# Decoder layer, one core: weight parts made by adding transfers, and a new order of stages

## The chip, the cores and the metric

The kernel runs on one core of one Trainium2 chip. The metric is the device time of one execution in microseconds (us); lower is better. The engines are named as in the profile: PE (TensorE, matmuls), DVE (VectorE), ACT (ScalarE), POOL (GpSimd) and SP (SyncE, which here only issues transfers).

## What is computed

One decoder layer over 2048 tokens of width 1024, in float32. Three parts follow each other, each added to the residual stream:

```python
h = rms_norm(x, mix_norm_g); z = h @ w_in                    # 1024 x 2048
y_lru = rg_lru(causal_dwconv(lru_x, ...), ...) * gelu(lru_gate)
c     = silu(layer_norm(causal_dwconv(conf_a * sigmoid(conf_b), 31 taps)))
x = x + concat([y_lru, c]) @ w_out

q = rms_norm(x, xa_norm_g) @ w_q                             # 4 heads of 256
k, v = split(rms_norm(mem, mem_norm_g) @ w_kv)               # 256 memory tokens
x = x + (softmax(q k^T / 16) v) @ w_o

g, u = split(rms_norm(x, ffn_norm_g) @ w_up)                 # 2 x 3072
x = x + (gelu(causal_dwconv(g, 3 taps)) * u) @ w_down
return rms_norm(x, final_norm_g)
```

## The kernel before

**Arithmetic.** TensorE multiplies in a rounded float32 format (`F32R`). To keep the precision, each operand is held as two tiles: the high part, which is the value rounded to `F32R`, and the low part, which is the rest. `split` makes them (ScalarE copies to the high part, VectorE subtracts it from the source), and `mm3` does three matmuls: high by high, high by low, low by high. Nearly all tiles are 128 x 512.

**The layer's stages.** The 2048 tokens go in four quarters of 512. `mixer(q)` computes the two mixing branches, `normed(q)` the layer norm of the convolution branch, `attend(q)` the output projection, the attention over the memory tokens and its output. Since the memory is the same for all tokens, two products of weights are folded ahead: `memory_a` makes `A` from the keys and `w_q`, and `memory_vo` makes `VO` from the values and `w_o`. Both are kept in device memory as high and low parts (`A_rows`, `VO_rows`, tensors `A2` and `VO2`). `memory_vo` takes, for each of four heads, two blocks of 128 rows of `w_o`; each block is loaded at once (`raw_rows`, 512 KB) and its two halves are split.

Quarters 2 and 3 (`FOLDED`) go through `attend_pair`, which multiplies 2 x 2 blocks with seven products instead of eight (`Folded`). For that it needs sums and differences of weight blocks, which `Folds.prepare` makes ahead for `w_out`, `A` and `VO`. `Folds.block` fetches one block: for `w_out` it is loaded from the input; for the other two, the high and the low part are read back by `Rows.get` and VectorE adds them. The FFN works the same way on halves of 1024 tokens (`HalfX`, `strassen_cols`, `up`, `Down`), with operands named `B11`, `B21`, `T2`, and so on, in `UP_ORDER`. `first_x` rounds and splits the first `EARLY` of these seven sets ahead of the first weight column; the rest is made when a product first asks for it (`HalfX.get`).

**The order.** Nothing is ordered by hand at the level of instructions. Each stage is a generator (`Task`); `drive` steps the first task in the list that is due, where a `yield n` makes the task due again after TensorE has been given n us of further work. `TURNS` is the list, first come first; the constants beside it (`MEM_WAIT`, `MIX_WAIT`, `PAIR_WAIT`, `FOLD_PACE` and others) are those n. This gives the order of the matmuls and of the buffers. `Program` then plans all engines: `deadlines` works out from TensorE's order when each operation is due, `schedule` plays the program through with estimated costs (`estimate`, `HOP`, `DMA_DELAY`, `DMA_RATE`, `ISSUE`) and takes on each engine the ready operation that is due first, and `emit` writes the best of three passes. On the chip each engine and each transfer queue then runs its list in that fixed order. 84 tiles of 128 x 512 (`S`) are shared by all stages and are granted in the order of their creation.

All recorded operations carry the line of `emit` (L399), so groups are told apart by tile names: `wl<-raw,wh` is the low part of a weight, `wd<-wh,wl` the sum in `Folds.block`.

Of the kernel before, what the change touches and what calls it, by code (L numbers as in the profile page):

```python
# [48 lines left out]


HOP = 0.3
HOP_SAME = 0.1
DMA_DELAY = 2.5
DMA_RATE = 300e3
ACT_SWITCH = 1.3
ACT_PATIENCE = 8.0
POOL_LAST = 6.0
# [75 lines left out]
class Program:  # L133
# [68 lines left out]
        o.calls.append((name, (out,) + args, kw))  # L202
        self.touch(o, [r.buf for r in ins] + list(reads), [r.buf for r in outs] + list(writes))

    def dma(self, out, in_, reads=(), writes=(), join=False, slack=30, by="SP"):


        o = self.op(by)
        o.moves = True
        refs = [r for r in (out, in_) if isinstance(r, Ref)]  # L210
        nbytes = max(int(np.prod(r.dummy.shape)) for r in refs) * 4
        o.cost, o.delay = nbytes / DMA_RATE, DMA_DELAY
        o.calls.append(("dma_start", (), dict(out=out, in_=in_)))
        rd = [in_.buf] if isinstance(in_, Ref) else []
        wr = [out.buf] if isinstance(out, Ref) else []
        o.store = slack if rd else False
        self.touch(o, rd + list(reads), wr + list(writes), join)
# [42 lines left out]
    def schedule(self):  # L260
        events, seq = [], [0]
        ready = {e: [] for e in self.engines}
        busy = {e: 0.0 for e in self.engines}
        idle = {e: True for e in self.engines}
        free = {t: list(range(n)) for t, n in SLOTS.items()}
        queues = {t: list(reversed(q)) for t, q in self.queues.items()}
        table, dma_free, lag = [None], {e: 0.0 for e in ISSUE}, [0.0]
        order = []

        def push(t, kind, x):  # L270
            seq[0] += 1
            heapq.heappush(events, (t, seq[0], kind, x))

        def satisfied(o, t):
            o.at = max(o.at, t)
            o.wait -= 1
            if o.wait == 0:
                push(o.at, 1, o)

        def grant(tag, t):  # L280
            while free[tag] and queues[tag]:
                b = queues[tag].pop()
                b.slot = free[tag].pop(0)
                b.left = len(b.ops)
                for o in b.heads:
                    satisfied(o, t)

        def pick(e, t):
            h = ready[e]
            while h and h[0][2].start is not None:  # L290
                heapq.heappop(h)
            if not h:
                return None
            if e == "Pool":
                back, o, wake = [], None, None
                while h and o is None:
                    x = heapq.heappop(h)
                    if x[2].start is not None:
                        continue
                    spare = x[2].due + lag[0] - POOL_LAST - t  # L300
                    if x[2].either and spare > 0:
                        back.append(x)
                        wake = spare if wake is None else min(wake, spare)
                    else:
                        o = x[2]
                for x in back:
                    heapq.heappush(h, x)
                if o is None and wake is not None:
                    push(t + max(wake, 0.2), 3, e)
                return o  # L310
            if e == "ACT":
                o = h[0][2]
                if o.sets is not None and table[0] not in o.sets and o.due + lag[0] - t > ACT_PATIENCE:
                    other = [x for x in h if x[2].sets is None or table[0] in x[2].sets]
                    if other:
                        x = min(other)
                        h.remove(x)
                        heapq.heapify(h)
                        return x[2]
            return heapq.heappop(h)[2]  # L320

        def dispatch(e, t):
            if not idle[e]:
                return
            o = pick(e, t)
            if o is None:
                return
            idle[e] = False
            o.start, o.on = t, e
            order.append(o)  # L330
            if e == "PE":
                lag[0] += 0.2 * (t - o.turn - lag[0])
            cost = o.cost
            if e == "ACT" and o.sets is not None and table[0] not in o.sets:
                cost += ACT_SWITCH
                table[0] = o.sets[0]
            if o.either and e == "DVE":
                cost = estimate("DVE", "tensor_tensor", 1024, False)
            if o.moves:
                dma_free[e] = max(dma_free[e], t) + cost  # L340
                push(t + ISSUE[e], 2, e)
                push(dma_free[e] + o.delay, 0, o)
            else:
                push(t + cost, 2, e)
                push(t + cost, 0, o)

        for o in self.ops:
            o.wait = len(o.preds) + 1
        for tag, queue in self.queues.items():
            for b in queue:  # L350
                for o in b.heads:
                    o.wait += 1
        for tag in SLOTS:
            grant(tag, 0.0)
        for o in self.ops:
            satisfied(o, 0.0)
        end = 0.0
        while events:
            t, _, kind, o = heapq.heappop(events)
            end = max(end, t)  # L360
            if kind == 1:
                for e in (["DVE", "Pool"] if o.either else [o.eng]):
                    heapq.heappush(ready[e], (o.due, o.idx, o))
                    dispatch(e, t)
            elif kind == 3:
                dispatch(o, t)
            elif kind == 2:
                idle[o] = True
                dispatch(o, t)
            else:  # L370
                for s in o.succs:
                    satisfied(s, t + (HOP_SAME if s.eng == o.on else HOP))
                for b in o.bufs:
                    b.left -= 1
                    if b.left == 0:
                        free[b.tag].append(b.slot)
                        grant(b.tag, t + HOP)
        assert len(order) == len(self.ops)
        self.estimated = end
        return order  # L380
# [42 lines left out]
def hybrid_layer(  # L423
# [154 lines left out]
    def split(src, hi, lo):  # L578
        ACT(hi[:], src, AF.Copy)
        V("tensor_tensor", lo[:], src, hi[:].f32(), op=ALU.subtract)  # L580

    def split_scaled(src, g, hi, lo):
        ACT(hi, src, AF.Copy, scale=g)
# [440 lines left out]
    def memory_vo():  # L1024
        yield mem_a
        yield VO_LATE
        for h in range(4):
# [1 line left out]
            yield 1  # L1029
            pp = [ps() for _ in range(4)]  # L1030
            for db in range(2):
                st = raw_rows(w_o[0], h * M + db * P)
                ww = []
                for half in range(2):
                    hi, lo = pair("w")
                    split(st[:, half * TT : (half + 1) * TT], hi, lo)
                    ww.append((hi, lo))
                for i, p in enumerate(pp):
                    mb, (wh, wl) = i // 2, ww[i % 2]
                    vs = slice(db * M + mb * P, db * M + (mb + 1) * P)  # L1040
                    with together():
                        mm3(p[:], vh[:, vs], vl[:, vs], wh[:], wl[:], db == 0, db == 1)
                    if i % 2:
                        yield 0
# [609 lines left out]
    class Folds:  # L1654
# [5 lines left out]
        def block(self, k, half):  # L1660
            if self.rows.w is not None:
                t = tmp("wd")
                pr.dma(t[:], self.rows.w[k * P : (k + 1) * P, half * TT : (half + 1) * TT])
                return t
            hi, lo = self.rows.get(k, half)
            t = tmp("wd")
            V("tensor_tensor", t[:], hi[:].f32(), lo[:].f32(), op=ALU.add)
            return t

        def prepare(self, wait):  # L1670
# [302 lines left out]
        yield V_LATE  # L1973
        vec["v3072"] = columns([ffn_conv_w[0], ffn_conv_b], DFF, "v3072")

    EARLY, VO_WAIT, V_LATE, Z_COPIED = 5, 2, 500, (0, 1)
    MIX_WAIT, MIX_TURN, LN_SUM, LN_SQ, GATES = (5, 7, 6, 0), 5, 6, 0, 3
    MIX_PACE, ATT_PACE = (1, 4, 3, 4), ((0, 3, 0), (0, 2, 2), (6, 3, 3), (5, 9, 0))
    PAUSE, WARM = 2, 16
    FED = ("B21", "T2", "T1", "T3")  # L1980
    MEM_WAIT, VO_LATE, ATT_TURN, FFN_TURN, X_PACE, T_PACE = 17, 10, 1, (3, 8, 7, 24), 3, 10

    FOLDED = (2, 3)
    PAIR_WAIT, PAIR_TURN, FOLD_PACE = (0, 0, 9, 17), 7, (6, 7, 35)
    EARLY_AT, KEPT_AT = 6, 5
    FOLD_AT = lambda: ([turned_x[0]], [mem_a, turned_x[1]], [mem_vo])
    F_out, F_a, F_vo = Folds(W_out, "t_out"), Folds(A_rows, "t_a"), Folds(VO_rows, "t_vo")

    NORMED = [lambda: ([m[0]], 108), lambda: ([attended[0]], 31), lambda: ([m[2]], 26), lambda: ([m[3], n[2]], 6)]
    ATTEND = [lambda: [n[0]], lambda: [n[1]]]  # L1990
    TURNS = lambda: [later, first, fold, m[0], mem_a, m[1], first_t, a[0], n[2], m[3], n[0], n[3], mem_vo, n[1], m[2], a[1], a[2], tail]
    X = [HalfX(h) for h in range(NH)]

    def first_x():
# [6 lines left out]
    def feed_forward():  # L2001
        yield first
        yield attended[NQ - 1]
        spawn(X[1].kept(attends[NQ - 1], 20), tail)
        spawn(prepare_down(), tail)
        yield from up(0, X[0], X[1].make)
        down = Down()
# [55 lines left out]
```

## Time and profile before

| | us |
|---|---|
| median of 3 runs | 2397.39 (2396.77 to 2397.78) |
| profiled execution: span from first to last instruction | 2396.1 |
| PE busy | 2382.6 |
| DVE busy | 2034.0 |
| ACT busy | 1313.2 |
| POOL busy | 11.2 |

For the profiled execution no time is given beside its span; the span lies 1.3 us under the median of the timed runs and 0.7 us under the fastest. A group's row reads: line, engine, operation, written tile <- read tiles, shape and count | busy us, mean ns of one | idle time just before them and what ended it. A row of one tile gives the durations as min/median/max in ns, and the first and the last start in us. `SPq` and `POOL` rows with DMA are the issue of a transfer; the issue rows give count, KB each and the median time from issue to landing. The granted TensorE clock was 0.999 over the span. The transfers moved 604.56 MB.

### The profile page before, as it was taken

Reading aid. Unit: us, or ns where it says so; the run is one execution under the profiler, and the core shown is the slowest. Engines: PE = TensorE matmul, PEld = TensorE weight load, DVE = VectorE, ACT = ScalarE, POOL = GpSimd, SP = SyncE. Lnnn points to the kernel's source line nnn. Section 1 sums busy time; section 2 is a strip of 40 time slices with the busy share of each in tenths; the row PEclk is TensorE's granted clock in tenths of the full one; section 3 lists DMA queues with packets and bytes.
Section 4 is the critical chain, followed back from the end, with each engine's and each line's share of the span. In section 5 each row is a group of like instructions: output and inputs, shape, how many; then the busy total and the mean of one; then the engine's idle time right before and its main releaser. Section 6 shows DMA issues by size and latency. Waiting matters only on the chain.

```text
span 2396.1 us, 33483 instructions
## 1 busy us (share of the span) xinstructions
PE 2382.6 (99%) x10948; PEld 1974.5 (82%) x10948; DVE 2034.0 (85%) x3355; ACT 1313.2 (55%) x2374; POOL 11.2 (0%) x26
## 2 busy tenths in 40 slices
PE   9999999999999999999999999999999999999998
PEld 7898888888887888888888888888888888888887
DVE  7999994299899869879999887988988896676787
ACT  7772776357557678695555555554555541222333
POOL 1000000000000000000000000000000000000000
PEclk9999999999999999999999999999999999999999
DMA  9598789775878988787766544556565589887986
GB/s 351 197 296 309 234 300 305 254 255 176 296 261 271 318 277 280 268 289 265 252 234 208 194 172 158 175 177 211 190 216 199 186 303 324 283 280 254 312 303 258
DMA packets 363912, 604.56 MB, mean 252 GB/s; under 512 B 34809, under 2 KB 116985, under 8 KB 363738
## 3 DMA queue, kind: packets, MB, share of 16 engines
q1 hardware_dynamic: 362952, 601.81, 73.8%
q8 instruction: 86, 1.41, 0.2%
q14 instruction: 88, 0.72, 0.1%
q0 software_dynamic: 640, 0.36, 0.0%
q10 hardware_dynamic: 146, 0.27, 0.0%
HBM read 409.36 MB, written 192.94 MB: 251 GB/s over the span
## 4 chain that ended last, share of the span: by engine, by line
PE 94%; DVE 2%; ACT 2%; DMA 1%; issue 1%; SPq 0%; POOL 0%; DVEq 0%; POOLq 0%; ACTq 0%
PE ps L399 94%; DMA wl<-w_down 1%; DVE conv L399 1%; ACT L399 0%; DMA raw<-in_w_kv_dram 0%; ACT wh L399 0%; DVE wl L399 0%; ACT gate L399 0%; DVE x L399 0%; DVE s L399 0%; ACT yh L399 0%; DVE smalls L399 0%; DVE ptl L399 0%; ACT prob L399 0%; ACT conv L399 0%
## 5 line engine op out<-in xcount | busy, mean ns | idle before, releaser
L399 PE MATMUL ps<-Xh,wh 128*128 128x512 f32 x1344 | 523.3, 389 | 0.7 <-ACT u L399 0.7
L399 PE MATMUL ps<-Xh,wl 128*128 128x512 f32 x1344 | 523.2, 389 | 0.7 <-DVE wl L399 0.5
L399 PE MATMUL ps<-Xl,wh 128*128 128x512 f32 x1344 | 523.0, 389 | 0.0
L399 PE MATMUL ps<-wh,hidh 128*128 128x512 f32 x960 | 374.4, 390 | 0.0
L399 PE MATMUL ps<-wh,hidl 128*128 128x512 f32 x960 | 374.2, 390 | 0.1
L399 PE MATMUL ps<-wl,hidh 128*128 128x512 f32 x960 | 373.7, 389 | 0.0
L399 DVE SCALAR_TENSOR_TENSOR conv<-cb,v,conv 128x512 f32<-128x512 f32 x480 | 334.9, 741 | 1.8 <-ACT conv L399 0.9
L399 PEld LDWEIGHTS ps<-Xh,wl 128*128 128x128 f32 x1344 | 252.3, 188 | 54.0 <-DVE wl L399 1.5
L399 PEld LDWEIGHTS ps<-Xh,wh 128*128 128x128 f32 x1344 | 252.3, 188 | 53.1 <-ACT u L399 1.1
L399 PEld LDWEIGHTS ps<-Xl,wh 128*128 128x128 f32 x1344 | 252.3, 188 | 52.5
L399 ACT ACTIVATE hidh<-s 128x512 fp32r<-128x512 f32 x186 | 113.8, 631 | 271.6 <-DVE s L399 227.9
L399 PEld LDWEIGHTS ps<-wh,hidl 128*128 128x128 f32 x960 | 180.2, 188 | 39.5 <-DVE hidl L399 2.1
L399 PEld LDWEIGHTS ps<-wh,hidh 128*128 128x128 f32 x960 | 180.2, 188 | 37.8 <-ACT hidh L399 0.4
L399 PEld LDWEIGHTS ps<-wl,hidh 128*128 128x128 f32 x960 | 180.3, 188 | 37.2 <-DMA wl<-w_down 0.4
L399 PE MATMUL ps<-xh,wh 128*128 128x512 f32 x512 | 204.0, 398 | 0.1
L399 PE MATMUL ps<-xl,wh 128*128 128x512 f32 x512 | 199.6, 390 | 0.3 <-DVE xl L399 0.3
L399 PE MATMUL ps<-xh,wl 128*128 128x512 f32 x512 | 199.6, 390 | 0.0
L399 ACT ACTIVATE wh<-s 128x512 fp32r<-128x512 f32 x192 | 119.6, 629 | 117.6 <-DVE s L399 79.1
L399 ACT ACTIVATE wh<-raw 128x512 fp32r<-128x512 f32 (+2 forms) x214 | 127.4, 613 | 53.1 <-PE ps L399 21.6
L399 ACT ACTIVATE u<-ps 128x512 f32<-128x512 f32 x144 | 85.7, 595 | 126.0 <-PE ps L399 125.2
L399 DVE TENSOR_TENSOR acc<-acc,ps 128x512 f32<-128x512 f32 (+1 forms) x157 | 102.7, 678 | 59.5 <-PE ps L399 56.4
L399 DVE TENSOR_TENSOR wl<-raw,wh 128x512 fp32r<-128x512 f32 (+2 forms) x214 | 140.2, 668 | 12.0 <-ACT wh L399 10.7
(256 smaller groups left out, 4014.2 us busy)
## 6 DMA issues: line engine op xcount, KB each, us to landing
raw<-in_w_up_dram SPq DMA_DIRECT2D x96, 512.0 KB, 4.5
wh<-w_down SPq DMA_DIRECT2D x156, 256.0 KB, 4.9
wl<-w_down SPq DMA_DIRECT2D x156, 256.0 KB, 5.0
w_down<-wh SPq DMA_DIRECT2D x144, 256.0 KB, 3.1
w_down<-wl SPq DMA_DIRECT2D x144, 256.0 KB, 3.5
h<-hid SPq DMA_DIRECT2D x120, 256.0 KB, 4.7
wh<-w_in SPq DMA_DIRECT2D x96, 256.0 KB, 4.2
wl<-w_in SPq DMA_DIRECT2D x96, 256.0 KB, 4.7
```

The costliest lines, as they stand in the source:

```text
L399: getattr(e, name)(*[resolve(a) for a in args], **{k: resolve(a) for k, a in kw.items()})
```

## The change

Three things:

1. In `memory_vo`, `split` of a loaded block of `w_o` becomes `split_fetched`. A transfer issued by POOL writes the high part directly from the input (rounding on the way), ScalarE writes its negative to the low part, and a second transfer from POOL adds the input to that. VectorE and the loaded copy have no part in it any more.
2. In `Folds.block`, for `A` and `VO`, the high part is read to the target by SP, and the low part is added to it by a transfer from POOL. Before, VectorE added two tiles that had been read.
3. The planner's transfers share one estimated stream with a delay of 3.5 us (it was one stream for each issuing engine, 2.5 us); and `TURNS` and the constants beside it have other values.

```diff
-HOP_SAME = 0.1
-DMA_DELAY = 2.5
-DMA_RATE = 300e3
+HOP_SAME = 0.05
+DMA_DELAY = 3.5
+DMA_RATE = 350e3
...
-    def dma(self, out, in_, reads=(), writes=(), join=False, slack=30, by="SP"):
+    def dma(self, out, in_, reads=(), writes=(), join=False, slack=30, by="SP", **more):
...
-        o.calls.append(("dma_start", (), dict(out=out, in_=in_)))
+        o.calls.append(("dma_start", (), dict(out=out, in_=in_, **more)))
...
-                dma_free[e] = max(dma_free[e], t) + cost
+                dma_free[0] = max(dma_free[0], t) + cost
                 push(t + ISSUE[e], 2, e)
-                push(dma_free[e] + o.delay, 0, o)
+                push(dma_free[0] + o.delay, 0, o)
...
+    def split_fetched(hi, lo, src):
+        pr.dma(hi[:], src, by="Pool")
+        ACT(lo[:], hi[:].f32(), AF.Copy, scale=-1.0)
+        pr.dma(lo[:], src, by="Pool", accum_op=ALU.add)
...
             for db in range(2):
-                st = raw_rows(w_o[0], h * M + db * P)
+                r0 = h * M + db * P
                 ww = []
                 for half in range(2):
                     hi, lo = pair("w")
-                    split(st[:, half * TT : (half + 1) * TT], hi, lo)
+                    split_fetched(hi, lo, w_o[0][r0 : r0 + P, half * TT : (half + 1) * TT])
...
-            hi, lo = self.rows.get(k, half)
+            kept, i = self.rows.kept, (k * 2 + half) * 2
             t = tmp("wd")
-            V("tensor_tensor", t[:], hi[:].f32(), lo[:].f32(), op=ALU.add)
+            pr.dma(t[:], kept.at(i), reads=[kept.tok[i]])
+            pr.dma(t[:], kept.at(i + 1), reads=[kept.tok[i + 1]], by="Pool", accum_op=ALU.add)
             return t
...
-    EARLY, VO_WAIT, V_LATE, Z_COPIED = 5, 2, 500, (0, 1)
-    MIX_WAIT, MIX_TURN, LN_SUM, LN_SQ, GATES = (5, 7, 6, 0), 5, 6, 0, 3
-    MIX_PACE, ATT_PACE = (1, 4, 3, 4), ((0, 3, 0), (0, 2, 2), (6, 3, 3), (5, 9, 0))
-    PAUSE, WARM = 2, 16
+    EARLY, VO_WAIT, V_LATE, Z_COPIED = 1, 1, 500, (0, 1)
+    MIX_WAIT, MIX_TURN, LN_SUM, LN_SQ, GATES = (3, 7, 10, 0), 5, 5, 0, 3
+    MIX_PACE, ATT_PACE = (2, 4, 3, 4), ((0, 3, 2), (0, 2, 2), (0, 0, 0), (0, 0, 0))
+    PAUSE, WARM = 1, 16
...
-    MEM_WAIT, VO_LATE, ATT_TURN, FFN_TURN, X_PACE, T_PACE = 17, 10, 1, (3, 8, 7, 24), 3, 10
+    MEM_WAIT, VO_LATE, ATT_TURN, FFN_TURN, X_PACE, T_PACE = 5, 11, 4, (6, 10, 0, 0), 0, 12
...
-    PAIR_WAIT, PAIR_TURN, FOLD_PACE = (0, 0, 9, 17), 7, (6, 7, 35)
+    PAIR_WAIT, PAIR_TURN, FOLD_PACE = (1, 0, 16, 36), 7, (8, 6, 35)
...
-    NORMED = [lambda: ([m[0]], 108), lambda: ([attended[0]], 31), lambda: ([m[2]], 26), lambda: ([m[3], n[2]], 6)]
+    NORMED = [lambda: ([m[0]], 108), lambda: ([attended[0]], 32), lambda: ([m[2]], 27), lambda: ([m[3], n[2]], 18)]
...
-    TURNS = lambda: [later, first, fold, m[0], mem_a, m[1], first_t, a[0], n[2], m[3], n[0], n[3], mem_vo, n[1], m[2], a[1], a[2], tail]
+    TURNS = lambda: [n[3], later, m[0], n[1], fold, mem_a, m[1], n[2], n[0], a[0], m[3], first, mem_vo, m[2], a[1], first_t, a[2], tail]
...
-        spawn(X[1].kept(attends[NQ - 1], 20), tail)
+        spawn(X[1].kept(attends[NQ - 1], 43), tail)
```

More of the change, by code (lines that the diff above doesn't have):

```diff
@@ L266, in schedule @@
         queues = {t: list(reversed(q)) for t, q in self.queues.items()}
-        table, dma_free, lag = [None], {e: 0.0 for e in ISSUE}, [0.0]
+        table, dma_free, lag = [None], [0.0], [0.0]
         order = []
```

## The prediction

> **What bounds the kernel now.** I read the page first, then busy time by stage, then what TensorE waited for. From the page: the span, the busy rows, and VectorE's slices (busy tenths, forty equal ones).
>
> ```profile
> span 2396.1 us, 33483 instructions
> PE 2382.6 (99%) x10948; PEld 1974.5 (82%) x10948; DVE 2034.0 (85%) x3355; ACT 1313.2 (55%) x2374; POOL 11.2 (0%) x26
> DVE  7999994299899869879999887988988896676787
> ```
>
> TensorE (PE) is busy in 2382.6 of 2396.1 us, so 13.5 us are all that any reordering can touch. By stretch (start:end, length, then busy us of PE, PEld, DVE, ACT, POOL, the granted clock, the transfer engines' share, GB/s):
>
> ```profile
> 0.00:2.41 2.41, 0.00 (x1) 0.01 (x1) 0.39 (x6) 1.10 (x1) 1.45 (x8) 1.00 0.09 25
> 2.41:60.00 57.59, 57.31 (x288) 47.77 (x289) 46.73 (x105) 43.08 (x90) 9.73 (x19) 1.00 1.03 365
> 60.00:300.00 240.00, 238.50 (x1217) 203.22 (x1216) 236.85 (x373) 145.29 (x265) 0.00 (x0) 1.00 0.77 259
> 300.00:360.00 60.00, 59.31 (x280) 48.09 (x279) 58.68 (x93) 46.11 (x83) 0.00 (x0) 1.00 0.87 302
> 700.00:780.00 80.00, 79.48 (x370) 63.67 (x369) 79.06 (x130) 66.66 (x113) 0.00 (x0) 1.00 0.81 276
> 1480.00:1530.00 50.00, 48.62 (x213) 39.27 (x212) 46.78 (x76) 32.58 (x55) 0.00 (x0) 1.00 0.55 184
> 2300.00:2389.50 89.50, 89.40 (x391) 72.68 (x389) 73.63 (x141) 38.48 (x89) 0.00 (x0) 1.00 0.82 302
> 2389.50:2396.13 6.63, 0.00 (x1) 0.00 (x0) 1.96 (x6) 2.03 (x6) 0.00 (x0) 0.77 0.42 158
> ```
>
> The first 2.41 us and the last 6.63 us hold no matmul, and the change edits neither. That leaves 13.5 - 2.4 - 6.6 = 4.5 us of idle TensorE in the middle: 0.28, 1.50, 0.69, 0.52, 1.38 and 0.10 us in the six stretches shown between, and 0.04 in the others. The waits of TensorE (writer, what it waited for, us, times, longest) name them; the first lies at the start:
>
> ```profile
> PE ps L399 <- POOL ident masks.py:199: 2.4, 1, 2.4
> PE ps L399 <- DMA raw<-in_w_kv_dram: 1.5, 1, 1.5
> PE ps L399 <- ACT u L399: 0.7, 1, 0.7
> PE ps L399 <- DVE wl L399: 0.5, 1, 0.5
> PE ps L399 <- DVE x L399: 0.5, 1, 0.5
> PE ps L399 <- DVE xl L399: 0.3, 1, 0.3
> PE ps L399 <- ACT prob L399: 0.3, 1, 0.3
> PE ps L399 <- DVE ptl L399: 0.2, 1, 0.2
> ```
>
> Where the first two of the middle lie, by the chain that ended last (start, length):
>
> ```profile
> 137.94 7.47 DMA raw<-in_w_kv_dram
> ...
> 353.30 0.61 DVE x L399
> ```
>
> These are slightly short of the truth. Matmuls start every 0.23 us and are recorded as 0.39 us long, so each wait can hide another 0.16 us. Timeline rows (start, length) of two matmuls and of the transfer that the first needs, and the same for the first use of the output weights; all serve below:
>
> ```profile
> 239.24 0.42 SPq L399 DMA_DIRECT2D raw<-in_w_o_dram  x1
> 252.68 0.39 PE L399 MATMUL ps<-wh,kvh 128*128 128x512 f32 x1
> 252.91 0.39 PE L399 MATMUL ps<-wl,kvh 128*128 128x512 f32 x1
> ...
> 159.62 1.07 SPq L399 DMA_DIRECT2D raw<-in_w_o_dram  x2
> L399 PE MATMUL ps<-wh,kvh x32: 389/389/390, 181.7 to 373.8; 128*128 128x512 f32 x32
> ```
>
> For the seven waits of the middle that is 7 x 0.16 = 1.1 us. All that can be won is about 4.5 + 1.1 = 5.6 us, 0.23% of the run. VectorE (DVE) is nearly as full as TensorE in 60-360 and 700-780 us (236.85 of 240, 58.68 of 60, 79.06 of 80), so its work can come late there; that is where the edit takes work from it.
>
> **The change, part by part.** (1) The output weights `w_o`. Four heads, two row blocks, two halves: 16 splits. Each loses a VectorE subtraction; its ScalarE copy stays as a copy scaled by -1; and 8 loads of 512 KB on SP become 32 transfers of 256 KB on POOL, half of them adding to their target. (2) The sums of kept parts of `A2` and `VO2`: 32 blocks, each losing a VectorE addition and one of two SP transfers, for one adding transfer on POOL. The rows: a subtraction like the 16, the 32 additions, the loads of w_o, a kept part, and what POOL has moved so far.
>
> ```profile
> L399 DVE TENSOR_TENSOR wl<-raw,wh 128x512 fp32r<-128x512 f32 x43 | 28.0, 681 | 0.6 <-ACT wh L399 0.5
> L399 DVE TENSOR_TENSOR wd<-wh,wl x32: 672/681/693, 609.0 to 963.3; 128x512 f32<-128x512 f32 x32
> raw<-in_w_o_dram SPq DMA_DIRECT2D x8, 512.0 KB, 6.7
> wl<-A SPq DMA_DIRECT2D x60, 256.0 KB, 4.9
> tmp<-in_lru_w_x_dram POOLq DMA_DIRECT2D x2, 64.0 KB, 5.9
> 12.70 1.25 POOL L399 DMA_DIRECT2D tmp<-in_lru_w_x_dram  x2
> ```
>
> VectorE is relieved of 48 x 0.68 = 33 us in all: 16 x 0.68 = 10.9 us ahead of 360 us, and 32 x 0.68 = 21.8 us spread over 609-963 us, of which 700-780 gets about 21.8 x 80 / 354 = 4.9 us. The bytes of w_o double, 4 MB more on some 605, where the transfer engines run at 0.77: nothing on the path unless the chain below is late.
>
> The price of the first part is a longer chain. Now it is load (6.7), copy (0.6), subtraction (0.7): 8.0 us. Afterwards it is rounding load, negating copy, adding load. No row shows an adding transfer or a 256 KB transfer by POOL. The nearest is POOL's 64 KB at 5.9 us, beside SP's 256 KB at 4.9, so 5.9 + 0.6 + 5.9 = 12.4 us. POOL takes 0.63 us to issue a transfer of 64 rows (1.25 for two); for 128 rows I take twice that, 1.3 us, and if it isn't within the 5.9 the chain is 15.0 us. Behind the adding transfer, which waits on POOL's queue for the copy, stand only the next w_o load and the sums, since POOL's list ends at 14 us today. 64 x 1.3 = 83 us of issue is no load in 2396. The tightest lead in the rows above, issue to matmul, is 252.68 - 239.24 = 13.4 us; the first loads, at 159.6 us, lead by 22 (181.7). So the chain fits at 12.4 and misses by 1.6 at 15.0; the planner counts POOL's issue and 3.5 us of delay, and can ask earlier. I take 0, between 0 and the price of the last rival. For the sums nobody hurries: they feed a product that is stored and read later. They cost nothing, and they free two of three tiles per block.
>
> [...]
>
> (3) The order. `MEM_WAIT` goes from 17 to 5, so the memory's keys and values start up to 12 us earlier, before the transfers of 120-200 us fill up; there the one wait on `w_kv` arose (1.5 us visible, 1.7 with its hidden part). Between all of it and none I take half: -0.8. `DVE x` at 354 us (0.5, 0.7 with the hidden part) follows directly on the 10.9 us of relief: all gone, -0.7. `ACT prob` and `DVE ptl` (0.3 and 0.2, with hidden 0.8) lie in 700-780, where 4.9 us of VectorE are freed: gone, -0.8. What is late next there is VectorE again, only less. The 1.38 us of 1480-1530 come from rounding the second half's activations during the last weights of the first half; nothing in the edit relieves that: 0. POOL's and SP's queues are passed by the moved tasks too, but 40 fewer SP issues leave room.
>
> `EARLY` goes from 5 to 1: of seven sets of rounded activations for the FFN, only one is asked for ahead of its first weight column. Each set is four splits, so up to 16 splits may move past the FFN's start at 1042.8 us.
>
> ```profile
> 1020.00:1043.00 23.00, 23.00 (x120) 19.60 (x119) 18.50 (x31) 22.19 (x45) 0.00 (x0) 1.00 0.72 256
> 1043.00:1063.00 20.00, 20.00 (x107) 17.09 (x106) 12.17 (x22) 18.78 (x36) 0.00 (x0) 1.00 0.89 299
> L399 DVE TENSOR_TENSOR Xl<-tx,Xh x16: 659/684/693, 1024.5 to 1054.3; 128x512 fp32r<-128x512 f32 x16
> L399 DVE TENSOR_TENSOR Xl<-xn,Xh x12: 681/683/693, 1013.0 to 1061.1; 128x512 fp32r<-128x512 f32 x12
> L399 PE MATMUL ps<-Xh,wh x1344: 388/389/500, 1042.8 to 1962.0; 128*128 128x512 f32 x192
> L399 ACT ACTIVATE wh<-s 128x512 fp32r<-128x512 f32 x192 | 119.6, 629 | 117.6 <-DVE s L399 79.1
> ```
>
> Here ScalarE is the tight one: 18.78 of 20 us, with 1.2 free. Sixteen copies of 0.63 us are 10.1, so 8.9 us uncovered if all of them move; none if the planner, which may run them as soon as tiles are free, leaves them where they are. The nearest case is the second half's set, made on the fly, at 1.38 us. I take half of that, +0.7, since the stage ahead is looser than the one at 1480.
>
> Sum: -0.8 - 0.7 - 0.8 + 0.7 = -1.6 us on the profiled 2396.1, so a span of 2394.5. The median of the runs, 2397.39, stands 1.3 above that profile; the prediction is 2397.39 - 1.6 = 2395.8 us.
>
> **The rivals.** *Waits change places.* A new order of 18 tasks and some 30 numbers removes the eight waits and makes eight others. For it: VectorE stays over 90% full in 60-300 after the relief (236.85 - 10.9 = 226 of 240), and the waits are single events of 0.2 to 1.5 us. The relief then isn't seen: 2397.4, give or take 1.5.
>
> *All waits go.* 2397.39 - 5.6 = 2391.8 us. Against it: more than half of the 5.6 lies at 145 us (a transfer) and at 1480-1530, where the edit takes nothing off an engine.
>
> *The FFN starts late* (slower). The mechanism is `EARLY`; the place is 1043-1063 us; the price reaches 8.9 us instead of 0.7: 2395.8 + 8.2 = 2404.0. It decides from 16 x 0.63 - 1.2 down to about 7.2 us uncovered (then the other gains no longer hold the total within 0.2%), that is, when some 13 of the 16 splits really move. Against it: the 28 splits of the seven sets already reach from 1013 to 1061 us today, ahead of and behind the start, with no wait of TensorE.
>
> *POOL's chain is late* (slower too). At 15.0 us, and behind one more issue of 1.3, a group with the tightest lead waits 2.9 us. If four of the eight groups have that lead, 11.6 us: 2407.4. It decides from about 6.5 us in all.
>
> Would a full VectorE hold POOL's issues up? At 12.70-13.95 us POOL issued at 0.63 us each beside a VectorE that ran the forms with two tensors which fill it where w_o is fetched:
>
> ```profile
> 11.99 1.41 DVE L399 SCALAR_TENSOR_TENSOR xl<-ps,vmix,xh 128x512 fp32r<-128x512 f32 x2 [0.34 <-ACT xh L399]
> 13.32 0.41 DVE L399 TENSOR_TENSOR wl<-raw,wh 128x256 fp32r<-128x256 f32 x1
> ```
>
> [...]
>
> **How the numbers follow.** A difference under 0.2% (4.8 us) can hardly be told from no change. Chances: the forecast 0.41, waits change places 0.28, all waits go 0.12, FFN late 0.11, POOL late 0.08. Faster by over 0.2% (below 2392.6) is only the third: 0.12. Slower (above 2402.2) is the last two, less 0.01 for a part that stays small: 0.18. The same: 0.70. The range goes from 2391.7 (all waits gone) to 2404.0 (FFN late in full); outside it remain POOL's chain and as much again for waits that I cannot name. The likeliest case alone is 2393.5 to 2397.5.
>
> **What would show it.** Right: VectorE's busy time about 33 us lower, as many matmuls as before, POOL with 64 more transfers; no wait on `DVE x` near 354 us or at 700-780; TensorE idle in the middle about 3 us. Wrong: TensorE waiting for `wl` or `wh` of w_o behind a transfer or ScalarE's negation near 160-375 us (POOL's chain); waits on `Xh` or `Xl` in the 20 us after the FFN's start (EARLY); adding transfers that land much later than 6 us; waits of a microsecond or more in stages that the edit doesn't touch, which would mean that the order, and not the transfers, made the time.

## The result, and the profile after

The changed kernel takes 2401.92 us (median of 21 runs, 2398.10 to 2406.06), the kernel before, timed beside it, 2397.39 (2395.80 to 2399.05). The ratio is 1.0019, interval 1.0013 to 1.0026: 4.5 us slower, where 1.6 us faster was forecast. Its runs spread over 8 us, those of the kernel before over 3.3. The profiled execution took 2398.55 us (span 2396.8), so it is one of the shorter ones: some 3.4 us of the median are not in it. A second profiled execution (e4 below) is 2.1 us longer.

From the page of the changed kernel, the span and the busy row:

```profile
span 2396.8 us, 33552 instructions
PE 2382.4 (99%) x10948; PEld 1975.9 (82%) x10948; DVE 2008.4 (84%) x3307; ACT 1303.1 (54%) x2368; POOL 62.5 (3%) x90
```

VectorE has the 48 instructions fewer that were forecast, POOL 64 transfers more, TensorE the same 10948. Busy time by stage, columns as in the prediction:

```profile
120.00:200.00 80.00, 80.00 (x490) 72.69 (x489) 79.01 (x124) 44.59 (x93) 8.99 (x13) 1.00 0.99 314
250.00:300.00 50.00, 48.74 (x220) 39.03 (x220) 49.84 (x79) 41.67 (x73) 0.00 (x0) 1.00 0.66 216
300.00:360.00 60.00, 60.00 (x285) 49.22 (x284) 54.09 (x85) 42.34 (x82) 5.78 (x8) 1.00 0.97 324
700.00:780.00 80.00, 77.92 (x356) 62.96 (x353) 71.46 (x117) 66.05 (x109) 4.37 (x5) 0.98 0.84 280
1043.00:1063.00 20.00, 20.00 (x106) 17.11 (x105) 14.20 (x25) 16.64 (x32) 0.00 (x0) 1.00 0.93 328
1480.00:1530.00 50.00, 50.00 (x223) 41.39 (x222) 45.02 (x74) 31.76 (x53) 0.00 (x0) 1.00 0.52 179
```

Three of the old holes are gone: the one at 145 us, the one at 354, and the 1.38 us of 1480-1530, which nothing was expected to touch. In 700-780 VectorE went from 79.06 to 71.46 us, and yet TensorE's idle time there went from 0.52 to 2.08. A new hole is in 250-300 (1.26 us). The same stretch of the kernel before was full:

```profile
250.00:300.00 50.00, 50.00 (x228) 40.45 (x227) 49.29 (x78) 40.43 (x70) 0.00 (x0) 1.00 0.74 239
```

What TensorE waited for in the changed kernel (the wait for `x` is new too and lies in the first 30 us; those for `xl` and `vol` are the hole in 250-300):

```profile
PE ps L399 <- POOL ident masks.py:199: 2.5, 1, 2.5
PE ps L399 <- DVE ptl L399: 2.1, 1, 2.1
PE ps L399 <- DMA x<-in_x_dram: 0.8, 1, 0.8
PE ps L399 <- DVE xl L399: 0.7, 1, 0.7
PE ps L399 <- DVE vol L399: 0.5, 1, 0.5
```

The wait of 2.1 us lies at 756 us. TensorE's rows there, and the six microseconds around them by busy time and clock:

```profile
755.04 1.03 PE L399 MATMUL ps<-ident,prob 128*128 128x128 f32 x8
758.16 1.11 PE L399 MATMUL ps<-ident,prob 128*128 128x128 f32 x4 [2.08 <-DVE ptl L399]
758.93 0.78 PE L399 MATMUL ps<-wh,pth 128*128 128x512 f32 x1
...
757.00:763.00 6.00, 4.84 (x19) 4.03 (x20) 3.60 (x6) 5.92 (x7) 0.72 (x1) 0.72 1.07 354
```

The wait costs twice. After it the granted clock is 0.72 over six microseconds, and matmuls of 512 columns, which start every 0.23 us ahead of the wait (753.45, 753.68), start every 0.43 us until about 761.5. The trace has the clock at one half for 3.41 us (0.50 from 758.11 to 761.52), so by estimate half of that, about 1.7 us, is lost on top of the 2.08. ScalarE's list in the same place shows what `ptl` (the low part of a turned probability, which needs the high part `pth`) waits for:

```profile
753.58 0.63 ACT L399 ACTIVATE m<-m 128x512 f32<-128x512 f32 x1
754.23 1.28 ACT L399 ACT_TABLE_LOAD   x1
755.52 0.72 ACT L399 ACTIVATE gate<-gate,nsp 128x512 f32<-128x512 f32 x1
756.15 0.61 ACT L399 ACTIVATE m<-xc 128x512 f32<-128x512 f32 x1
756.79 1.08 ACT L399 ACTIVATE pth<-ps 128x512 fp32r<-128x512 f32 x2
757.89 1.28 ACT L399 ACT_TABLE_LOAD   x1
```

The first four transposes end at about 755.6; the copy of their result starts at 756.79, behind a table load and two activations of a gate. TensorE's next transposes wait 2.08 us for `ptl`, which reads that result too (the bracket in their row). The engine that is late is ScalarE, which is busy only 66.05 of 80 us: it seems to have the wrong order and not too much work, which h1 below tests.

The transfers, by count, size and median time from issue to landing:

```profile
wh<-in_w_o_dram POOLq DMA_DIRECT2D x16, 256.0 KB, 6.7
wl<-in_w_o_dram POOLq DMA_DIRECT2D x16, 256.0 KB, 7.3
wd<-A POOLq DMA_DIRECT2D x16, 256.0 KB, 5.9
wd<-VO POOLq DMA_DIRECT2D x16, 256.0 KB, 7.5
...
L399 POOL DMA_DIRECT2D wl<-in_w_o_dram x16 | 14.3, 949 | 30.6 <-ACT wl L399 17.2 <-ACT ctail L399 7.4 <-ACT cb L399 5.9
```

### The profile page after: what moved, and what is told of

It is laid out like the page before. It is cut to its first block, busy times and chain, and to the rows that moved or that the text cites. A ratio compares the mean times of both kernels' runs of the same rounds, so it can differ in the third digit from the quotient of the medians.

```text
span 2396.8 us, 33552 instructions
## 1 busy us (share of the span) xinstructions
PE 2382.4 (99%) x10948; PEld 1975.9 (82%) x10948; DVE 2008.4 (84%) x3307; ACT 1303.1 (54%) x2368; POOL 62.5 (3%) x90
## 4 chain that ended last, share of the span: by engine, by line
PE 91%; DVE 6%; DMA 1%; ACT 1%; issue 1%; SPq 0%; POOL 0%; DVEq 0%; POOLq 0%; ACTq 0%
PE ps L399 91%; DVE conv L399 4%; DMA x<-in_x_dram 0%; DMA wd<-VO 0%; DVE al L399 0%; DVE qtl L399 0%; DVE xl L399 0%; SPq L399 0%; ACT gate L399 0%; DVE vol L399 0%; ACT L399 0%; DVE kvl L399 0%; DVE gate L399 0%; DVE xc L399 0%; DVE smalls L399 0%
## 5 line engine op out<-in xcount | busy, mean ns | idle before, releaser
L399 DVE TENSOR_TENSOR wl<-s,wh 128x512 fp32r<-128x512 f32 x192 | 130.0, 685 | 15.3 <-ACT wh L399 9.5
L399 ACT ACTIVATE wh<-raw 128x512 fp32r<-128x512 f32 (+2 forms) x198 | 117.6, 612 | 43.1 <-PE ps L399 17.1
L399 DVE TENSOR_TENSOR wl<-raw,wh 128x512 fp32r<-128x512 f32 (+2 forms) x198 | 130.1, 668 | 10.8 <-ACT wh L399 10.6
```

Source lines behind the costliest of these rows:

```text
L399: getattr(e, name)(*[resolve(a) for a in args], **{k: resolve(a) for k, a in kw.items()})
```

## The experiments

The change has three parts: the planner's numbers (`HOP_SAME`, `DMA_DELAY`, `DMA_RATE`, one estimated stream), the order of stages (`TURNS` and the constants beside it), and the transfers. The first runs take them apart. Below, *lost time* over a stage is worked out from the starts of the matmuls: how much the distances from one to the next exceed the usual distance of that kind in the kernel before, added up. It holds waits and slow clock alike. How much it is depends on what is called usual; its differences between runs are good to about half a microsecond.

**e1_order_only**: the changed kernel with the old data path.

```diff
-                    split_fetched(hi, lo, w_o[0][r0 : r0 + P, half * TT : (half + 1) * TT])
+                    split(st[:, half * TT : (half + 1) * TT], hi, lo)
...
-            pr.dma(t[:], kept.at(i + 1), reads=[kept.tok[i + 1]], by="Pool", accum_op=ALU.add)
+            V("tensor_tensor", t[:], hi[:].f32(), lo[:].f32(), op=ALU.add)
```

> The changed kernel's order of stages and planner numbers, with the old data path: w_o loaded and split with VectorE, the kept parts summed by VectorE, no adding transfer. Theory 1 (the new order made the time, the adding transfers are free): 2400 to 2404 us, ratio to the kernel before 1.0012 to 1.0027, single runs spread over 6 us or more as in the changed kernel (2398.1 to 2406.1). Theory 2 (the adding transfers land at varying times and hold something up): 2394 to 2398 us, runs spread over no more than 4 us as before (2395.8 to 2399.1).

Measured: 2406.39 us (2403.29 to 2406.97), ratio 1.0035 (1.0021 to 1.0049). That is above both expectations. New order and new numbers alone cost 9.0 us; the transfers then give 4.5 back.

**e2_transfers_only**: the kernel before with both kinds of adding transfer, old order, old numbers (the diff's `split_fetched` and `Folds.block`, nothing else).

> The kernel before with both kinds of adding transfers and nothing else (old order of stages, old planner numbers). Theory 1: 2394 to 2398 us, spread up to 4 us. Theory 2: 2400 us or more, spread 6 us or more; the old planner assumes a delay of 2.5 us for a transfer that takes 6 to 7, so it would be worse than the changed kernel.

Measured: 2432.08 us (2429.19 to 2439.04), ratio 1.0150 (1.0136 to 1.0164). By themselves the transfers cost 34.7 us. The waits of ScalarE and TensorE name a cause:

```profile
ACT wl L399 <- DMA wh<-in_w_o_dram: 46.7, 12, 11.1
...
PE ps L399 <- DVE xl L399: 8.4, 5, 3.5
PE ps L399 <- ACT xh L399: 6.5, 3, 3.6
```

ScalarE's negating copy (`wl`) waits 46.7 us for POOL's load. TensorE does not wait for `wh` or `wl` of `w_o` at all; it waits for activations that have nothing to do with `w_o`.

**e3_wo_by_vector**: the changed kernel, but `w_o` is split by VectorE as before; only the sums are made by transfers.

> The changed kernel with w_o loaded and split by VectorE again; the sums of kept parts still by adding transfers. Theory 1: as the changed kernel, 2400 to 2404 us. Theory 2, the w_o chain being what holds up (wl of w_o lands 7.3 us after issue, twice in a row): 2394 to 2398 us. Theory 2, the sums being what holds up: 2400 us or more.

Measured: 2402.07 us (2400.95 to 2406.24), ratio 1.0022 (1.0012 to 1.0032). By the medians the sums by transfer gain 4.3 us against e1 (the two intervals overlap); against the changed kernel, `w_o` by transfer gains nothing that can be told from zero.

**e4_changed_again**: the changed kernel once more, beside e1 to e3.

> The changed kernel, for a second profiled execution: the one shown took 2398.55 us and the median was 2401.92, so the typical execution's extra 3.4 us are not in that trace. Both theories: median 2400 to 2404 us. Theory 1: the extra is a wait of TensorE for VectorE or ScalarE, followed by matmuls at half the clock, as at 757-763 us. Theory 2: a wait within 20 us behind a transfer issued by POOL.

Measured: 2401.36 us (2397.03 to 2404.35), ratio 1.0015 (1.0006 to 1.0024). Its profiled execution, 2.1 us longer than the other, has the wait for `ptl` at 2.7 us and one more, of 1.4 us for `xh`, at 261 us:

```profile
761.39 0.66 PE L399 MATMUL ps<-ident,prob 128*128 128x128 f32 x4 [2.71 <-DVE ptl L399]
```

As far as two executions can show it, the same two places hold the loss, and the extra lies mostly at 261 us: TensorE is busy in 47.34 of the 50 us of 250-300, against 48.74. The slow matmuls that were expected did not come: the clock stayed at 1.00. 740-780 loses about 4 us in both.

**f1_transfers_told** and **f2_changed_told**: e2 and the changed kernel, with the planner told 6.0 us for POOL's transfers.

```diff
-        o.cost, o.delay = nbytes / DMA_RATE, DMA_DELAY
+        o.cost, o.delay = nbytes / DMA_RATE, (6.0 if by == "Pool" else DMA_DELAY)
```

> The kernel before with both kinds of adding transfers (2432 us in the run above), and one number more: the planner takes 6.0 us of delay for a transfer from POOL instead of 2.5, as the measured 6.9 us from issue to landing ask. Theory A (the loss is a wait put into ScalarE's list: the negating copy stands ahead of other work and waits for a load that comes 4 us later than planned; 46.7 us of such waits in 12 times): these waits fall under 10 us and the time to 2396 to 2404 us. Theory B (any new plan of this crowded program lies some 5 to 40 us above the tuned one, whatever the transfers do): over 2410 us.

> The changed kernel with 6.0 us of delay for a transfer from POOL instead of 3.5. Theory A: the remaining waits of ScalarE for w_o (7.5 and 9.5 us in the two traces) go, the loss in 250-300 us of 1.6 to 3.1 us with them: 2396 to 2400 us, runs within 5 us. Theory B: above 2402 us, since this order was tuned for another number.

Measured: f1 2408.08 us (2406.65 to 2408.99), ratio 1.0045 (1.0031 to 1.0059); f2 2401.84 (2397.02 to 2405.87), ratio 1.0019 (1.0010 to 1.0028). Both times lie between the two expectations. One number in the planner removes 24 of the 34.7 us, less than expected. ScalarE's wait for the load of `w_o`, first in f1, then in f2 (7.5 us in the changed kernel):

```profile
ACT wl L399 <- DMA wh<-in_w_o_dram: 21.5, 8, 4.4
...
ACT wl L399 <- DMA wh<-in_w_o_dram: 2.9, 2, 2.3
```

In the changed kernel the wait falls from 7.5 to 2.9 us and the time stays, so what is left of that wait costs nothing there.

**f3_planner_only** and **f4_turns_only**: the kernel before with the new planner numbers alone, and with the new order of stages alone.

> The kernel before with the planner's new numbers alone (delay 3.5 us, one stream at 350 GB/s, same-engine hop 0.05); old order of stages and old data path. The order without the transfers lost 9 us (2406.4). If the planner's numbers carry that loss: 2403 us or more. If the stages' order carries it: 2395 to 2399 us.

> The kernel before with the new constants and list of stages alone; old planner numbers, old data path. If the stages' order carries the 9 us: 2403 us or more, with the wait of TensorE on ptl near 760 us as in the changed kernel. If the planner's numbers do: 2395 to 2399 us, and no such wait. If both are above 2402, each was fitted to the other.

Measured: f3 2405.36 us (2404.47 to 2406.69), ratio 1.0036 (1.0023 to 1.0048); f4 2399.44 (2398.46 to 2403.52), ratio 1.0010 (1.0001 to 1.0019). Without transfers the new numbers cost 8 us and the new order 2. TensorE's wait for `ptl` near 760 us is 1.3 us in f4 and absent in f3. With the new numbers and the new order together it is there with the transfers and without them: 3.3 us in e1, 2.7 in e3, 2.5 in f2.

**g1_wo_only, g2_wo_negated_by_pool, g3_sums_only**: the two halves of e2, and a `w_o` chain that keeps off ScalarE's list.

```diff
# g2, against g1
-        ACT(lo[:], hi[:].f32(), AF.Copy, scale=-1.0)
+        pr.do("Pool", "tensor_scalar", lo[:], hi[:].f32(), -1.0, None, op0=ALU.mult)
```

> The kernel before with only w_o's lower parts made by adding transfers (old order, old planner numbers; the sums stay VectorE additions). It separates the two halves of e2_transfers_only, which took 34.7 us more. Theory A (the negating copy at the head of ScalarE's list waits for POOL's rounding load, and what stands behind it comes late to TensorE): TensorE loses about 15 us before 420 us and nothing later, 2410 to 2416 us, with ScalarE waiting some 45 us for that load. Rival B (the adding transfers themselves are what is late, lower part to matmul): the same time, but TensorE then waits for wl itself. Rival C (the sums make all of the loss): 2396 to 2400.

> As g1_wo_only, but the negation is done by POOL between its two transfers instead of by ScalarE, so nothing of ScalarE's list waits for a POOL transfer; the chain itself is not shorter. Theory A: the loss of g1 goes almost wholly, 2396 to 2402 us, and ScalarE's waits for the load are gone. Rival B (the chain's own length): the loss stays, 2408 to 2416 or more. Between them, 2402 to 2408, the issue of POOL, now held up by its own copy, would be late.

Measured: g1 2409.2 us (2406.96 to 2413.31), ratio 1.0050 (1.0037 to 1.0063); g2 2402.22 (2400.73 to 2403.12; an eleventh execution took 8597.57, which is not in the ratio and of which no trace was kept), ratio 1.0020 (1.0011 to 1.0030). Both are just outside their ranges, g1 below 2410 and g2 above 2402. Between 150 and 420 us the kernel before loses 2.7 us, g1 18.4, g2 7.4. Timeline rows of g1 at one place, on ScalarE, VectorE and TensorE, in brackets the idle time before and what ended it:

```profile
172.80 0.63 ACT L399 ACTIVATE wl<-wh 128x512 fp32r<-128x512 f32 x1 [3.03 <-DMA wh<-in_w_o_dram]
173.34 3.56 ACT L399 ACTIVATE xh<-ps,vmix 128x512 fp32r<-128x512 f32 x6
...
174.04 3.38 DVE L399 SCALAR_TENSOR_TENSOR xl<-ps,vmix,xh 128x512 fp32r<-128x512 f32 x5 [2.78 <-ACT xh L399]
...
174.85 1.31 PE L399 MATMUL ps<-ident,x 128*128 128x128 f32 x8 [2.77 <-DVE xl L399]
...
172.00:180.00 8.00, 5.23 (x20) 4.13 (x20) 5.76 (x10) 5.91 (x11) 0.89 (x1) 0.79 1.09 332
```

Read it downwards: the negation waits 3.03 us for its load at the head of ScalarE's list; six `xh` stand behind it; VectorE waits 2.78 us for the first of them; TensorE 2.77 us for VectorE, and the eight microseconds run at a clock of 0.79. The first matmul with `w_o` starts only at 184.9. In g2 the wait is POOL's:

```profile
L399 POOL TENSOR_SCALAR wl<-wh 128x512 fp32r<-128x512 f32 x16 | 32.2, 2018 | 41.1 <-DMA wh<-in_w_o_dram 32.5 <-DVE conv L399 5.0 <-PE ps L399 2.6
```

POOL stands idle 32.5 us for the same loads and takes 2.02 us for a negation, so the chain is longer than in g1, and yet 7.0 of g1's 12.3 us are gone. So that part of the loss came from what the waiting instruction holds up, and not from the length of the chain. The 5.3 us that remain are not explained.

> The kernel before with only the sums of kept parts made by adding transfers (old order, old planner numbers). Theory A (the planner places the additions' consumers as if the transfer took what SP's took, and VectorE's list waits for wd): VectorE waits some 10 us for wd in 600 to 960 us, and TensorE loses about 20 us after 620: 2413 to 2422 us. Rival (the sums gain, as they do under the new order, where they were worth 4.3 us): 2391 to 2398, and then the loss of e2 after 620 us would be an effect of the plan that the first half shifted.

Measured: 2418.96 us (2414.03 to 2420.92), ratio 1.0085 (1.0072 to 1.0099). From 620 to 780 us the kernel before loses 2.6 us, g3 20.8. It is the same thing on VectorE, where the prediction had that nobody hurries; timeline rows of VectorE and TensorE, and the stretch:

```profile
691.06 0.69 DVE L399 TENSOR_TENSOR t<-wd,t 128x512 f32<-128x512 f32 x1 [1.90 <-DMA wd<-A]
...
704.26 1.40 DVE L399 SCALAR_TENSOR_TENSOR xc<-z,v,xc 128x512 f32<-128x512 f32 x2
707.86 0.69 DVE L399 TENSOR_TENSOR t<-wd 128x512 f32<-128x512 f32 x1 [2.20 <-issue]
708.47 0.75 DVE L399 SCALAR_TENSOR_TENSOR xc<-z,v,xc 128x512 f32<-128x512 f32 x1
709.13 0.68 DVE L399 TENSOR_TENSOR xl<-xc,xh 128x512 fp32r<-128x512 f32 x1
...
705.72 0.79 PE L399 MATMUL ps<-xh,gwh 64*128 64x512 f32 x2 [3.69 <-ACT xh L399]
709.87 0.79 PE L399 MATMUL ps<-xl,gwh 64*128 64x512 f32 x2 [3.36 <-DVE xl L399]
...
703.00:715.00 12.00, 5.92 (x18) 3.44 (x18) 9.80 (x17) 5.04 (x7) 0.87 (x1) 0.57 0.88 244
```

The `t` of 707.86 needs the sum `wd`, whose adding transfer POOL issued at 699.70. The profile names no releaser in its bracket (`issue`). POOL's adding transfers from `A` landed 6.8 us after issue in this run (median; 2.4 to 9.5 for all transfers to `wd`), which puts this landing at an estimated 706.5, so it is the likely releaser and not a shown one. VectorE idles 2.20 us there, in a stage where it is the full engine (79.06 of 80 us in the kernel before), with `xc` and `xl` behind it; TensorE's 3.36 us follow. The 3.69 us before lie ahead of this wait; VectorE had already stood 1.90 us for another such sum at 691.06, with fifteen convolution steps and then `xc` behind it. TensorE is busy in 5.92 of 12 us.

**h3_sums_told**: g3 with 6.0 us told, as in f1.

> The kernel before with only the sums made by transfers (as g3_sums_only, 2419.0 us) and 6.0 us told as the delay of POOL's transfers. Theory A (VectorE's list waits at its head for a sum that the planner believed landed): 18 us or more of the 22 go, 2396 to 2401 us, and TensorE's loss at 700 to 780 us falls from 18 us to under 4. Rival (the transfers' traffic or POOL's issue is what costs): 2410 us or more.

Measured: 2401.52 us (2399.81 to 2403.07), ratio 1.0019 (1.0010 to 1.0027). 17.4 of the 22.0 us go, a little less than expected.

**g4_changed_old_planner** and **h4_old_turns**: the two corners still missing.

> The changed kernel with the planner's old numbers (0.05, 3.5 us, 350 GB/s, one queue for all transfers) under the new order of stages, with the adding transfers. Theory A (new planner numbers cost 8 us and are only paid back because they suit the new transfers): with the old numbers the transfers come late again, 2410 to 2430 us. Rival (the numbers cost in any case, the order of stages is what suits the transfers): 2394 to 2398 us, better than the changed kernel.

> The kernel before with both kinds of adding transfers and the planner's new numbers, under the old order of stages: the missing corner. If the planner's numbers are what makes the transfers bearable (3.5 us and one queue put a POOL transfer's planned landing later), 2400 to 2408 us, close to the changed kernel; if the order of stages does it, 2420 to 2432.

(The numbers in brackets in the first of these are the new ones; the run has the old ones, 0.1, 2.5 us, 300 GB/s and a stream for each engine.) Measured: g4 2429.26 us (2427.21 to 2432.22), ratio 1.0132 (1.0119 to 1.0146); h4 2406.58 (2403.02 to 2414.42), ratio 1.0048 (1.0034 to 1.0062). All eight corners, in us:

| planner's numbers | order | no transfers | transfers |
|---|---|---|---|
| old | old | 2397.4 (before) | 2432.1 (e2) |
| old | new | 2399.4 (f4) | 2429.3 (g4) |
| new | old | 2405.4 (f3) | 2406.6 (h4) |
| new | new | 2406.4 (e1) | 2401.9 (changed) |

With the old numbers the transfers cost 30 to 35 us under either order; with the new ones 1 us, or a gain of 4.5. So the numbers decide. They put a POOL transfer's landing later (0.87 + 2.5 us after issue before, 0.75 + 3.5 and behind all other transfers now, 5.9 to 7.5 measured), and ScalarE's wait for the loads of `w_o` is 41.7 us in g4 against 7.5 in the changed kernel. The later landing is not all of it: told alone, it takes back 24 of 34.7 us (f1) and, in the next run, 17 of 32.

**h2_turns_told**: the changed kernel with the old numbers, but 6.0 us told for POOL's transfers.

> The changed kernel with the planner's old numbers and queues, but 6.0 us told as the delay of a POOL transfer (2.5 us for all others). Theory A (the old numbers are better for all that is no POOL transfer, worth 7 to 8 us, and telling cures the lists' heads): 2393 to 2397 us, better than both kernels. Rival (the plan's new numbers help by chance of the order, no law in them): anything from 2398 to 2408, with waits of TensorE in other places.

Measured: 2412.06 us (2407.78 to 2416.53), ratio 1.0061 (1.0049 to 1.0073). A miss. Telling takes 17 of g4's 32 us away, but the old numbers are not better for the rest: the largest wait is now 3.4 us for `DVE x`. What a number does to a plan of this size was not to be had by reasoning.

**h1_two_gates_later**: the changed kernel, with three operations moved in the order that it emits: the two gate activations of 755.52 and 756.15 and the product of theirs go behind the two copies to `pth` and the GELU after them, which also saves a table load (six from 746 to 763 us, where the changed kernel has seven). The lists of TensorE, POOL and SP stay as they are.

```diff
-        _, order, places, slots = best
+        _, order, places, slots = best; late = [o for o in order if o.idx in (3085, 3086, 3087)]; ...
+        at = [o.idx for o in order].index(3121) + 1; order[at:at] = late
```

> The changed kernel with two activations of a gate (and the product of theirs on VectorE) put behind two copies of turned probabilities and one GELU in the emitted order near 756 us; TensorE's, POOL's and SP's lists are the same, ScalarE has one table load less. Theory A (TensorE's wait of 2.1 us there, and the 4 us at half clock behind it, come from the copies standing behind the gate's table load): the wait falls below 1 us, the clock stays up, and the time falls by 2.5 to 3.8 us, to 2398.0 to 2399.5. Rival (another bank or operand is then late in its place): 2401 to 2402.5, the wait still there with another releaser.

Measured: 2398.87 us (2395.10 to 2401.97), ratio 1.0006 (0.9997 to 1.0014): 3.0 us off the changed kernel's time, as expected (the two intervals just touch). TensorE's row, and the same six microseconds as above:

```profile
757.31 0.66 PE L399 MATMUL ps<-ident,prob 128*128 128x128 f32 x4 [1.30 <-DVE ptl L399]
...
757.00:763.00 6.00, 5.69 (x29) 4.78 (x30) 3.40 (x6) 5.93 (x8) 0.87 (x1) 1.00 1.05 354
```

The wait falls from 2.08 to 1.30, not below 1 as expected, and the clock stays at 1.00. Twenty-nine matmuls start where nineteen did. In 740-780 the lost time goes from 4.2 to 1.9 us.

**i1_two_places**: h1, and three steps of the convolution on VectorE put behind the `xc`, `xl` and `vol` that TensorE waits for at 261 us (the same kind of edit).

> h1_two_gates_later with three convolution steps on VectorE (0.66 us each) put behind the values that TensorE waits for at 261 us; nothing else moves. Theory A (the order of VectorE's list at that place costs 1.3 us, and up to 2.7 in slower executions): both waits there go, TensorE's loss in 250 to 300 us falls from 2.3 to about 1 us, and the time falls by 1.3 to 2.5 us, to 2396.4 to 2397.6: level with the kernel before. Rival (the time between h1 and before lies in other executions' waits, or the convolutions then come late): 2398 to 2400.

Measured: 2397.63 us (2394.08 to 2401.11), ratio 1.0000 (0.9991 to 1.0009). That is 1.2 us off h1, a little less than expected and not clear of the noise by itself (the intervals of h1 and i1 overlap). Both moves together are: the interval of i1 and that of the changed kernel no longer meet. The stretch 250-300, and the wait that is left there:

```profile
250.00:300.00 50.00, 49.49 (x224) 39.73 (x223) 49.78 (x78) 40.97 (x72) 0.00 (x0) 1.00 0.67 222
...
PE ps L399 <- DVE xl L399: 0.5, 1, 0.5
```

So the version with both moves is level with the kernel before. None of these kernels beats it.

## Why the prediction was wrong

**The sum.** Its terms under the order were -0.8 - 0.7 - 0.8 + 0.7 = -1.6 us (two of them, -0.7 and -0.8, count on VectorE's relief by the transfers), and the price of the transfers was 0. Measured, the order with the planner's numbers is +9.0 (e1), and the transfers on top of it -4.5. Both are wrong; the sum of the two, +4.5, lies on the other side of no change from the forecast. That it is still under the upper end of the range (2404.0) is luck: that end stood for `EARLY`, which cost nothing.

**The step that failed first: the order is read from the old waits alone.** The text took each old wait, asked whether it would go, and priced what is late next at nothing or a fraction. Two of three did go (`w_kv` at 145, `DVE x` at 354), and 1480-1530 too, which was booked at 0. But the sentence on 700-780, that what is late next there "is VectorE again, only less", was wrong. VectorE got its relief (79.06 to 71.46 us) and ScalarE became late, by the order of its list. The term of -0.8 became a hole of 2.08 us, 1.56 more than before, and the low clock behind it nearly doubled the price in the profiled execution. The hole at 261 us (1.26) had no term at all. These two places carry the loss: i1 takes 4.3 of the 4.5 us away by moving six operations and nothing else. That is shown. How the 4.3 divide between the two places is less sure: 3.0 and 1.2 by the medians, the 1.2 within the noise. Nor did the relief make the hole: e1, without transfers, has it too, at 3.3 us. Why the new numbers and the new order together bring it is not settled; f3 and h2 only show that changing the numbers moves the time by several microseconds.

**The rival that came true** is *waits change places*. It was given 2397.4 "give or take 1.5", a price of nil, because the old waits were "single events of 0.2 to 1.5 us". The size was off: taking 0.78 us and the low clock from the wait at 756 us was worth 3.0 (h1), and 2.08 us with the 1.7 of the clock make 3.8.

**The transfers.** The chain was estimated at 12.4 us and priced at 0. Measured, it is 6.7 + 0.6 + 7.3 = 14.6, near the bound of 15.0; POOL's issue took 0.95 us for such an adding transfer, not 1.3. TensorE never waited for it. What failed here is another step: "Behind the adding transfer, which waits on POOL's queue for the copy, stand only the next w_o load and the sums" asks what stands behind the chain on POOL, and not what stands behind the negating copy on ScalarE, which waits for the load. g1 and g2 show that this costs 7 us of 12, g3 that the same holds for the sums on VectorE ("nobody hurries", 22 us). In the changed kernel the planner's later landing happens to keep these waits at the heads of the lists short (41.7 us in g4, 7.5 here). In the traces of g1 and g3 ScalarE and VectorE stood still for 3.03 and 2.20 us with such an operation at the head of the list and other work behind it.

**What held.** VectorE lost 48 instructions; its busy time fell by 25.6 us where 33 were forecast. In part that is because successive rows overlap (0.69 us long, 0.61 apart at 707.86 in g3); the rest is not explained. `EARLY` cost nothing: 1043-1063 is full, 20.00 of 20, with 16.64 us of ScalarE where 18.78 was before. The rival *POOL's chain is late* did not come: no wait of TensorE for `wh` or `wl` of `w_o`. And the last line of the prediction named what came, waits of a microsecond or more in stages that the edit does not touch.

## What to carry to other kernels

When an operation comes to wait for a transfer, look at the list of the engine that runs it, not at the one that needs its result: in g1 and g3 what stood behind it on that engine waited too (3.03 us on ScalarE, 2.20 us on VectorE), and it was work of quite another stage in g1 (`xh`, which has nothing to do with `w_o`). A planner that is told a landing too early puts such an operation too early; measure the landing of a new kind of transfer and tell it. In a kernel that keeps TensorE at 99%, relief of a full engine is worth what the next hole costs, and that hole is found in the trace of after, not before: two moves by hand at the places that the waits name won back 4.3 of the 4.5 us that the whole change had cost.

## What the runs showed of the hardware

A wait of 2.08 us (the changed kernel, 756 us) was followed by 3.41 us at half clock, which makes 0.72 over 757-763; one of 1.30 us at the same place (h1) by a clock of 1.00 over the same six microseconds. The length of a wait alone doesn't decide: after e4's wait of 2.71 us, which ends at 761.39, the clock was 1.00 (757-763 and 758-764), with matmuls of 512 columns 0.23 us apart. What does decide was not shown. So a wait of two microseconds or more at this place cost an estimated 1.7 us more in one execution (half of 3.41) and nothing more in another.

A table load took 1.28 us in the changed kernel (mean of 69), and the activation behind the one of 754.23 started at once (754.23 + 1.28 = 755.51, start at 755.52).

A transfer of 256 KB by POOL landed 5.9 to 7.5 us after its issue in the changed kernel (medians), against 4.1 to 5.6 for the parts of `A` and `VO` that SP fetches. Its issue took 0.56 us for a load that rounds and 0.91 to 0.97 us for one that adds (means).
